# Seven block products in place of eight for the down projection of the first feed-forward block, in three chunks of six feature tiles and a plain chunk of four

## The chip, the cores and the metric

The kernel runs on one core of a Trainium2 chip. A core has a matrix engine (TensorE, PE in the profile; PEld is its loading of weights), a vector engine (VectorE, DVE), an activation engine (ScalarE, ACT), a general engine (GpSimd, POOL) and SyncE (SP), which only issues transfers. Each works through its own queue of instructions in order; they wait for each other by semaphores. SBUF holds operands, PSUM takes the sums of matmuls. The metric is the device time of one launch in microseconds.

## The reference

One step of a decoder trunk: a half-step SwiGLU feed-forward block, a mixer (pooling and a state-space scan), and a second feed-forward block, each behind an RMS norm, with residual adds. There are 512 prompt rows and 8 sample rows, 520 tokens in all, width 1024, feed-forward width 2816. Only the first feed-forward block is touched:

```python
def _swiglu(x, wg, wu, wd):
    return (jax.nn.silu(x @ wg) * (x @ wu)) @ wd
...
h = h + 0.5 * _swiglu(_rms_norm(h, ffn1_norm[l]), ffn1_w_gate[l], ffn1_w_up[l], ffn1_w_down[l])
```

The product with `wd` is the down projection: 2816 features in, 1024 out, for 520 tokens.

## The kernel before

Activations lie features on partitions, tokens along the free axis: `h` is 8 tiles of 128 features by 520 tokens. Tokens are split into two halves of 260 (`HB`). The 2816 inner features are 22 tiles of 128.

**Precision.** Each float32 operand is split into a rounded high part and a remainder, the low part. `mm3` (L122) forms a product as three matmuls: high by high, high by low, low by high. `split` (L102) makes the two parts of a weight: the high part by a copy on ACT (L107), the low part by a subtraction on DVE (L114), and, for a part of the columns called `late`, by ACT writing the negated high value (L110) and an accumulating DMA on POOL's queue adding the weight to it (L111).

**Gate and up products.** For each feature tile `f` the two weights (gate, up) and the two token halves form a 2 by 2 block problem, with the contraction in two halves as well. `Ffn.product` (L274) forms it by seven block products in place of eight (Winograd's variant of Strassen's scheme), numbered 1 to 7, each of 4 contraction tiles times 3 matmuls, so 84 matmuls to a tile. `load` (L255) fetches the weights and makes the combined ones: `s1` and `s2` by three additions on DVE (L266 to L268), then the splits of the plain and combined weights (`d1`, `e1`, `e2`, `d2`). The activations' seven combinations are made once, in `prep_pair` (L191), and kept in `xth` and `xtl`. Products that enter more than one output are copied out of PSUM to `ac` by ACT (L294) on the way. `gates` (L298) adds, scales by the norm factor and applies silu; `close` (L305) finishes the tile and splits the result into `g`, a high and a low part. The first two tiles of the block (`direct` = 2) are formed plainly during startup (`plain`, L226, `plain_out`, L241).

**Down products.** `rest` (L315) works through three chunks of 8, 8 and 6 feature tiles (`CHUNKS`). When a chunk's gates are done, `down` (L347) forms its share of the down projection for each of the 8 output tiles `d`: for each token half and each feature tile of the chunk one `mm3`, into two PSUM banks. `done` then scales the sum by -0.5 and the norm factor (L364) and adds it to `h` (L368). In the last chunk `after` also prepares the mixer's input of each finished output tile (`prep`, L141: a copy on ACT, a subtraction on DVE, L145, a square on ACT, L155, an add on DVE, L156).

**Order.** The gate product of the next chunk's first tiles is begun before a chunk's down products, so that TensorE is not left without work. Within these bounds the order of instructions on each engine is laid out ahead by a planner that runs on a cost model and takes work by priority and readiness. Buffers bound how far ahead it can go: two pairs of raw weights (`raw`), three high and low weight tiles (`whi`, `wlo`), two of each for combined weights (`sw`, `shi`, `slo`), three of `ac`, two of `tg`, and in PSUM two banks `A` and two pairs of banks `BE`. `g` has nine.

The second feed-forward block uses the same class, with `direct` = 1 and its own end (`down_by_half`).

Of the kernel before, what the change touches and what calls it, by code (L numbers as in the profile page):

```python
# [33 lines left out]
CHUNKS = (8, 8, 6)  # L34
# [28 lines left out]
def tile_trunk_step(ctx: ExitStack, tc: tile.TileContext, ins: dict, outs: dict):  # L63
# [120 lines left out]
    def scaled(gp, nb, norm, j, name):  # L184
        xg = gp.tile([P, 4, HB], F32, tag="g", bufs=nb, name=f"xg_{name}{j}")
        for d, out in ((j, xg[:, 0::3]), (j + KD // 2, xg[:, 1:3])):
            nc.scalar.activation(out=out, in_=h[:, d].rearrange("p (b t) -> p b t", b=2), func=AF.Copy,  # L187
                                 scale=v(norm, d))
        return xg

    def prep_pair(nx, gp, nb, xg, j, name):  # L191
        xth, xtl, _, _ = nx
        xd = gp.tile([P, 4, HB], F32, tag="g", bufs=nb, name=f"xd_{name}{j}")
        nc.vector.tensor_tensor(out=xd[:, 0:2], in0=xg[:, 0::2], in1=xg[:, 3:4].to_broadcast([P, 2, HB]),
                                op=ALU.subtract)
        nc.vector.scalar_tensor_tensor(out=xd[:, 2], in0=xd[:, 1], scalar=-1.0, in1=xg[:, 0], op0=ALU.mult,
                                       op1=ALU.subtract)
        nc.vector.scalar_tensor_tensor(out=xd[:, 3], in0=xd[:, 2], scalar=-1.0, in1=xg[:, 1], op0=ALU.mult,
                                       op1=ALU.subtract)
        for s, t in ((xg[:, 0:3], slice(0, 3)), (xd, slice(3, 7))):  # L200
            nc.scalar.copy(xth[:, j, t], s)
            nc.vector.tensor_tensor(out=xtl[:, j, t], in0=s, in1=xth[:, j, t].bitcast(F32), op=ALU.subtract)

    class Ffn:
# [4 lines left out]
        def __init__(self, nx, i, wx, gp, direct):  # L209
            self.nx, self.i, self.wx, self.gp, self.direct = nx, i, wx, gp, direct  # L210
            self.states = None
            self.w, self.A, self.BE, self.ac, self.g, self.tg, self.raw, self.banks, self.behind = ({} for _ in range(9))

# [12 lines left out]
        def plain(self, f, xg, j, us=(0, 1)):  # L226
            for u in us:
                if (f, u) not in self.banks:
                    n = f"P{self.i}_{f}{u}"
                    if f == 1 and u == 0:  # L230
                        bs = [ps[0].tile([P, 512], F32, tag="A", bufs=2, name=f"{n}{b}") for b in range(2)]
                    else:
                        t = ps[0].tile([P, 2, 512], F32, tag="BE", bufs=2, name=n)
                        bs = [t[:, 0], t[:, 1]]
                    self.banks[f, u] = bs
# [5 lines left out]
        def plain_out(self, f):  # L241
            tg = self.wx.tile([P, 2, HB], F32, tag="tg", bufs=2, name=f"tg{self.i}_{f}")
            g = self.g[f] = self.gp.tile([P, 2, 2, HB], F32R, tag="g", bufs=NG, name=f"g{self.i}_{f}")
# [4 lines left out]
            for b in range(2):  # L248
                nc.vector.scalar_tensor_tensor(out=tg[:, b], in0=self.banks[f, 1][b][:, :HB], scalar=-1.0, in1=tg[:, b],
                                               op0=ALU.mult, op1=ALU.mult)  # L250
            nc.scalar.copy(g[:, 0], tg)
            nc.vector.tensor_tensor(out=g[:, 1], in0=tg, in1=g[:, 0].bitcast(F32), op=ALU.subtract)
            return free.ins

        def load(self, f):  # L255
            i, wx, src = self.i, self.wx, ins[f"w{self.i}gu"]
            n = f"{i}_{f}"
            raw = raw_pair(n)
            nc.sync.dma_start(out=raw[:, 0], in_=src[2 * f])
            nc.sync.dma_start(out=raw[:, 1], in_=src[2 * f + 1])  # L260
            d1 = split(raw[:, 0], 1024, f"{n}a", wp, 3, ("whi", "wlo"), src[2 * f, :, 512:])
            s1 = wx.tile([P, 2, 512], F32, tag="sw", bufs=2, name=f"s1_{n}")
            s2 = wx.tile([P, 2, 512], F32, tag="sw", bufs=2, name=f"s2_{n}")
            up0 = raw[:, 1, :512].unsqueeze(1).to_broadcast([P, 2, 512])
            diag = bass.AP(up0.tensor, up0.offset - 1024, [up0.ap[0], (1536, 2), up0.ap[2]])
            nc.vector.tensor_tensor(out=s1, in0=diag, in1=up0, op=ALU.add)  # L266
            nc.vector.tensor_tensor(out=s2[:, 0], in0=s1[:, 1], in1=raw[:, 0, :512], op=ALU.add)
            nc.vector.tensor_tensor(out=s2[:, 1], in0=s2[:, 0], in1=raw[:, 0, 512:], op=ALU.add)  # L268
            e1 = split(s1.rearrange("p q c -> p (q c)"), 1024, f"{n}c", wx, 2, ("shi", "slo"))
            e2 = split(s2.rearrange("p q c -> p (q c)"), 1024, f"{n}d", wx, 2, ("shi", "slo"))  # L270
            d2 = split(raw[:, 1, 512:], 512, f"{n}b", wp, 3, ("whi", "wlo"), src[2 * f + 1, :, 512:])
            self.w[f] = {1: (d1, 0), 2: (d1, 4), 7: (e1, 0), 5: (e1, 4), 6: (e2, 0), 3: (e2, 4), 4: (d2, 0)}

        def product(self, f, p):  # L274
            js = range(KD // 2)
            if f not in self.A:
                with tc.issue_after(self.behind[f]) if f in self.behind else nullcontext():
                    self.load(f)
                n = f"{self.i}_{f}"
                self.A[f] = ps[0].tile([P, 512], F32, tag="A", bufs=2, name=f"A{n}")  # L280
                self.BE[f] = ps[0].tile([P, 2, 512], F32, tag="BE", bufs=2, name=f"BE{n}")
                self.ac[f] = [self.wx.tile([P, 2, HB], F32, tag="ac", bufs=3, name=f"ac{n}_{q}") for q in range(2)]
            slot, dst, opens = {1: (0, 0, True), 2: (1, 1, True), 5: (3, 2, True), 6: (5, 0, False),
                                3: (2, 2, False), 7: (4, 0, False), 4: (6, 0, False)}[p]
            out = self.A[f] if dst == 0 else self.BE[f][:, dst - 1]
            (whi, wlo), k0 = self.w[f][p]
            xth, xtl = self.nx[:2]
            for j in js:
                mm3(out[:, :HB], ws(whi, k0 + j), ws(wlo, k0 + j), xth[:, j, slot], xtl[:, j, slot], opens and j == 0,
                    j == KD // 2 - 1, skip_group_check=True)  # L290
            a, c = self.ac[f]
# [6 lines left out]
        def gates(self, f):  # L298
            tg = self.tg[f] = self.wx.tile([P, 2, HB], F32, tag="tg", bufs=2, name=f"tg{self.i}_{f}")
            nc.vector.tensor_tensor(out=tg, in0=self.BE[f][:, :, :HB], in1=self.ac[f][0], op=ALU.add)  # L300
            nc.vector.tensor_tensor(out=tg, in0=tg, in1=self.nx[3].rearrange("p (b t) -> p b t", b=2), op=ALU.mult)
            nc.scalar.activation(out=tg, in_=tg, func=AF.Silu)
            nc.vector.tensor_tensor(out=tg[:, 1], in0=self.ac[f][1][:, 0], in1=tg[:, 1], op=ALU.mult)

        def close(self, f):  # L305
            tg = self.tg[f]
            nc.vector.tensor_tensor(out=tg[:, 0], in0=self.A[f][:, :HB], in1=tg[:, 0], op=ALU.mult)
            g = self.g[f] = self.gp.tile([P, 2, 2, HB], F32R, tag="g", bufs=NG, name=f"g{self.i}_{f}")
            nc.scalar.copy(g[:, 0], tg)  # L309
            nc.vector.tensor_tensor(out=g[:, 1], in0=tg, in1=g[:, 0].bitcast(F32), op=ALU.subtract)  # L310
# [3 lines left out]

        def rest(self, before, last_chunk):  # L315
            lo = 0
            for c, n in enumerate(CHUNKS):
                hi = lo + n
                last = hi == KF
                for f in range(self.direct if c == 0 else lo + 1, hi if last else hi + 1):  # L320
                    self.step(f)
                if last:
                    self.product(KF - 1, 4)
                    with tc.high_priority():
                        self.close(KF - 1)
                    wd = before()
                else:
                    self.product(hi + 1, 1)
                    self.product(hi, 4)
                    self.close(hi)  # L330
# [4 lines left out]
                lo = hi  # L335

        def step(self, f):
            if f not in self.A:
                self.product(f, 1)
            if f - 1 not in self.g and f > self.direct:  # L340
                self.product(f - 1, 4)
                self.close(f - 1)
            for p in (2, 5, 6, 3, 7) if f == KF - 1 else (5, 6, 3, 7, 2):
                self.product(f, p)
            self.gates(f)
# [93 lines left out]
    wx1, g1 = pool("wx1", "right"), pool("g1", "right")  # L439
    ffn_psum("ppf1")  # L440
    nx1 = new_xt(xt1, "f1")
    ffn1 = Ffn(nx1, 1, wx1, g1, 2)
    xg1 = []
    for j in range(KD // 2):
# [4 lines left out]
        xg1.append(scaled(g1, NG, "ffn1_norm", j, "f1"))  # L449
# [4 lines left out]
        prep_pair(nx1, g1, NG, xg1[j], j, "f1")  # L454
    ffn1.plain_load(1)
    with tc.high_priority():
        ffn1.scales()
    for u in range(2):
        for j in range(KD // 2):
            ffn1.plain(1, xg1[j], j, (u,))  # L460
    with tc.high_priority():
        ffn1.behind[2] = ffn1.plain_out(0)
    ffn1.plain_out(1)
# [19 lines left out]
    def open_f2():  # L483
# [4 lines left out]
        f2["ffn"] = Ffn(new_xt(f2["xt"], "f2"), 2, f2["wx"], None, 1)  # L488

    def fin(d, b, hs):  # L490
# [5 lines left out]
        if j >= 0 and b:  # L496
            f2[j] = scaled(f2["xg"], 4, "ffn2_norm", j, "f2")

    def fill(j):
# [3 lines left out]
        prep_pair(f2["ffn"].nx, f2["xg"], 4, f2[j], j, "f2")  # L503
# [611 lines left out]
```

## Time and profile before

| | us |
|---|---|
| median of 3 runs | 1008.37 (1007.89 to 1009.1) |
| profiled execution | 1008.41 |
| its span, first to last instruction | 1006.5 |
| mean granted TensorE clock | 0.996 |

The first feed-forward block fills about the first 372 us of the span: the first matmul of startup starts at 5.25, the first down product at 112.0 and the last at 371.2, and the mixer's first matmul (`dt`) at 372.36. In rows of instructions the columns are the start, the duration, the engine, the line, the operation, the result and its operands, the shape and the count; in brackets stands the time for which the engine was idle before it and what ended that. In rows of busy time by stage the columns are the stretch, its length, then for PE, PEld, DVE, ACT and POOL the busy time and, in brackets, the number of instructions, then the granted TensorE clock, the DMA engines' share and GB/s. A matmul's printed duration (about 283 ns) is its latency; matmuls overlap, so what one costs is the distance from one start to the next.

### The profile page before, as it was taken

What the parts mean: (1) busy time and instruction counts of PE and PEld (TensorE: products, weight loads), DVE (VectorE), ACT (ScalarE), POOL (GpSimd) and SP (SyncE); (2) the same over time, 40 slices, a digit from 0 to 9 for tenths busy, and PEclk for the clock granted to TensorE, in tenths of its full rate; (3) what the DMA queues carried; (4) which work ended last, traced back from release to release, by engine and by line L of the source; (5) the groups of instructions that cost most, each with busy time, mean ns of one, the idle gap of its engine ahead of it and who ended that gap; (6) DMA issues with size and microseconds to landing.
All of it is one profiled execution on the core that took longest, in us unless ns stands there. A gap on an engine that the chain in (4) does not pass through costs nothing.

```text
span 1006.5 us, 19720 instructions
## 1 busy us (share of the span) xinstructions
PE 976.0 (97%) x7852; PEld 952.8 (95%) x7852; DVE 766.7 (76%) x1366; ACT 564.4 (56%) x961; POOL 157.3 (16%) x239
## 2 busy tenths in 40 slices
PE   7999999999999999999999999999999999999996
PEld 6899999999999999999899998899999999999995
DVE  7788556886468688789979987998857788477776
ACT  7677415765137455685754325677644676535653
POOL 0111001110011000156411000111212211122100
PEclk9999999999999999999999999999999999999998
DMA  5566424754345332263335322456646766556612
GB/s 185 166 167 163 111 99 116 178 137 117 126 110 135 93 124 97 90 192 100 121 122 159 117 86 95 127 131 175 140 139 185 210 151 165 131 179 171 144 64 85
DMA packets 53835, 135.97 MB, mean 135 GB/s; under 512 B 7720, under 2 KB 14824, under 8 KB 53744
## 3 DMA queue, kind: packets, MB, share of 16 engines
q1 hardware_dynamic: 38864, 103.78, 31.8%
q0 software_dynamic: 14880, 30.94, 16.0%
q8 instruction: 61, 1.00, 0.4%
q14 instruction: 30, 0.25, 0.1%
HBM read 127.36 MB, written 7.34 MB: 134 GB/s over the span
## 4 chain that ended last, share of the span: by engine, by line
PE 85%; DVE 6%; ACT 5%; issue 2%; DMA 2%; POOL 1%; SPq 0%; DVEq 0%; ACTq 0%; POOLq 0%
PE A L123 8%; PE A L126 7%; PE A L127 7%; PE dn L127 7%; PE dn L123 6%; PE dn L126 6%; PE BE L123 6%; PE BE L127 6%; PE BE L126 6%; PE P L238 3%; PE wo L123 2%; PE wo L126 2%; PE wo L127 2%; PE inz L123 2%; PE inz L127 2%
## 5 line engine op out<-in xcount | busy, mean ns | idle before, releaser
L123 PE MATMUL dn<-g,whi_1d 128*128 128x260 f32 x352 | 99.5, 283 | 1.8 <-ACT whi_1d L107 1.6
L126 PE MATMUL dn<-g,whi_1d 128*128 128x260 f32 x352 | 99.5, 283 | 0.0
L127 PE MATMUL dn<-g,wlo_1d 128*128 128x260 f32 x352 | 99.0, 282 | 0.0
L364 DVE SCALAR_TENSOR_TENSOR td<-dn,r_f 128x520 f32<-128x520 f32 x40 | 27.9, 699 | 91.7 <-PE dn L127 91.7
L127 PE MATMUL dn<-g,wlo_2d 128*128 128x260 f32 x256 | 72.8, 284 | 2.0 <-DVE wlo_2d L114 2.0
L123 PE MATMUL dn<-g,whi_2d 128*128 128x260 f32 x256 | 72.4, 283 | 0.1
L126 PE MATMUL dn<-g,whi_2d 128*128 128x260 f32 x256 | 72.3, 282 | 0.0
L123 PEld LDWEIGHTS dn<-g,whi_1d 128*128 128x128 f32 x352 | 66.1, 188 | 2.4 <-ACT whi_1d L107 2.0
L126 PEld LDWEIGHTS dn<-g,whi_1d 128*128 128x128 f32 x352 | 66.3, 188 | 0.0
L127 PEld LDWEIGHTS dn<-g,wlo_1d 128*128 128x128 f32 x352 | 66.1, 188 | 0.0
L107 ACT CAST whi_1d<-raw_1d 128x1024 fp32r<-128x1024 f32 (+1 forms) x24 | 23.4, 979 | 70.4 <-PE dn L126 62.2
L294 ACT COPY ac<-A 128x260 f32<-128x260 f32 x123 | 44.0, 371 | 17.1 <-PE A L127 17.1
L266 DVE TENSOR_TENSOR s<-raw 128x1024 f32<-128x1024 f32 x41 | 49.9, 1218 | 3.3 <-DMA raw<-in_w2gu 3.3
L238 PE MATMUL P<-xg_f,raw 128*128 128x260 f32 x192 | 45.6, 396 | 5.3 <-DMA raw<-in_w1gu 5.3
L127 PEld LDWEIGHTS dn<-g,wlo_2d 128*128 128x128 f32 x256 | 48.2, 188 | 2.6 <-DVE wlo_2d L114 2.6
L123 PEld LDWEIGHTS dn<-g,whi_2d 128*128 128x128 f32 x256 | 48.3, 189 | 0.3 <-ACT whi_2d L107 0.3
L126 PEld LDWEIGHTS dn<-g,whi_2d 128*128 128x128 f32 x256 | 48.2, 188 | 0.0
L238 PEld LDWEIGHTS P<-xg_f,raw 128*128 128x128 f32 x192 | 37.4, 198 | 11.2 <-ACT xg_f L187 5.2
L126 PE MATMUL wo<-catg,whi_wo 128*128 128x260 f32 x128 | 36.4, 285 | 1.3 <-DVE catg L972 1.3
L123 PE MATMUL wo<-catg,whi_wo 128*128 128x260 f32 x128 | 37.3, 292 | 0.3 <-DVE h L941 0.3
L310 DVE TENSOR_TENSOR g<-tg,g 128x520 fp32r<-128x520 f32 x41 | 28.6, 698 | 11.6 <-ACT g L309 11.6
L123 PE MATMUL inz<-xh_mx,whi_inz 128*128 128x260 f32 x128 | 36.8, 287 | 0.1
(1442 smaller groups left out, 4001.2 us busy)
## 6 DMA issues: line engine op xcount, KB each, us to landing
raw<-in_w2gu SPq DMA_DIRECT2D x44, 512.0 KB, 4.7
raw<-in_w1gu SPq DMA_DIRECT2D x42, 512.0 KB, 4.5
raw_1d<-in_w1d SPq DMA_DIRECT2D x16, 512.0 KB, 4.4
raw_2d<-in_w2d SPq DMA_DIRECT2D x16, 512.0 KB, 5.7
raw_wo<-in_w_out SPq DMA_DIRECT2D x12, 512.0 KB, 4.5
ab<-scr_acs SPq DMA_DIRECT2D x8, 512.0 KB, 4.4
h<-in_state_ssm SPq DMA_DIRECT2D x16, 256.0 KB, 4.1
raw_inz<-in_w_in SPq DMA_DIRECT2D x8, 512.0 KB, 4.3
```

The source lines that it names most:

```text
L107: nc.scalar.copy(h, src)
L123: first = nc.tensor.matmul(ps, whi, xhi, start=start, stop=False, **kw)
L126: nc.tensor.matmul(ps, whi, xlo, start=False, stop=False, **kw)
L127: nc.tensor.matmul(ps, wlo, xhi, start=False, stop=stop, **kw)
L238: nc.tensor.matmul(self.banks[f, u][b][:, :HB], ws(self.raw[f][:, u], j + 4 * q), xg[:, slot[q]], start=j == q == 0, stop=j == 3 and q == ...
L266: nc.vector.tensor_tensor(out=s1, in0=diag, in1=up0, op=ALU.add)
L294: nc.scalar.copy(keep, out[:, :HB])
L310: nc.vector.tensor_tensor(out=g[:, 1], in0=tg, in1=g[:, 0].bitcast(F32), op=ALU.subtract)
L364: nc.vector.scalar_tensor_tensor(out=t, in0=banks[d][:, :, :HB], scalar=-0.5, in1=self.nx[3].rearrange("p (b t) -> p b t", b=2), op0=ALU.mult,
```

## The change

The down projection of the first block is formed by the same seven products, for 18 of its 22 feature tiles. Chunks are now 6, 6, 6 and 4 tiles; `paired` = 3 says that the first three chunks go the new way. The second block keeps its chunks of 8, 8 and 6 and `paired` = 0.

- Within a paired chunk the feature tiles are worked in the order lo, lo+3, lo+1, lo+4, lo+2, lo+5. Two tiles in a row form a pair, "first" and "second": the two halves of the contraction of a block problem.
- The first tile's result is held in the tile `acc` (`gx`). When the second closes, `g_split` makes four differences on DVE and splits all seven combinations into high and low parts (three copies on ACT, three subtractions on DVE), in a tile `gt` of 14 x 260 columns; there are three of them, one for each pair of a chunk.
- A down step `(c, d)` takes the place of the plain down products of output tiles `d` and `d+1`: the two output tiles and the two token halves are the block problem. It goes through the same `load`, `product`, `gates` and `close` as a feature tile, with weights of 768 columns in place of 1024 and 3 contraction tiles in place of 4, so 63 matmuls in place of 72. Its `gates` and `close` scale and add to `h` instead of forming silu. There are 4 such steps to a chunk, 12 in all.
- The next chunk's first tile is stepped through before the down steps. Its result waits in `acc` until its partner closes; where the next chunk is the plain one (role "late"), `g_plain` splits it there.
- The last chunk has 4 feature tiles, and its down products are formed plainly, as before, with `after` for the mixer.
- At startup the plain tiles are 0 and 3, and the block's `xg` and `xd` tiles come from a pool of their own (`xo`), released before the pool of `gt` is opened.

```diff
-CHUNKS = (8, 8, 6)
+CHUNKS = {1: (6, 6, 6, 4), 2: (8, 8, 6)}
...
+                if c < paired:
+                    fs = [lo + q * (n // 2) + k for k in range(n // 2) for q in range(2)]
...
+        def g_homes(self, f):
+            t = self.tg[f]
+            if self.role(f) in ("first", "late"):
+                t = act.tile([P, NT], F32, tag="acc", name=f"gx{self.i}_{f}").rearrange("p (b t) -> p b t", b=2)
+                self.gx = t
+            self.out[f] = t
...
+        def g_split(self, f):
...
+            gx, go = self.gx, self.out[f]
+            self.gx = None
+            t = self.gt[f] = self.gp.tile([P, 14, HB], F32R, tag="gt", bufs=3, name=f"gt{self.i}_{f}")
+            xd = self.gp.tile([P, 4, HB], F32, tag="xd", name=f"gd{self.i}_{f}")
+            nc.vector.tensor_tensor(out=xd[:, 0], in0=gx[:, 0], in1=gx[:, 1], op=ALU.subtract)
+            nc.vector.tensor_tensor(out=xd[:, 1], in0=go[:, 1], in1=gx[:, 1], op=ALU.subtract)
+            nc.vector.scalar_tensor_tensor(out=xd[:, 2], in0=xd[:, 1], scalar=-1.0, in1=gx[:, 0], op0=ALU.mult,
+                                           op1=ALU.subtract)
+            nc.vector.scalar_tensor_tensor(out=xd[:, 3], in0=xd[:, 2], scalar=-1.0, in1=go[:, 0], op0=ALU.mult,
+                                           op1=ALU.subtract)
+            for x, q in ((gx[:, 0], 0), (go, slice(1, 3)), (xd, slice(3, 7))):
+                hi, lo = t[:, 0:7][:, q], t[:, 7:14][:, q]
+                nc.scalar.copy(hi, x)
+                nc.vector.tensor_tensor(out=lo, in0=x, in1=hi.bitcast(F32), op=ALU.subtract)
...
+        def load(self, k):
+            i, wx = self.i, self.wx
+            if isinstance(k, tuple):
+                c, d = k
+                fs = self.chunks[c]
+                n, src = f"{i}d{d}_{c}", ins[f"w{i}d"][d : d + 2, :, min(fs) * P : (max(fs) + 1) * P]
...
+            n = len(self.chunks[k[0]]) // 2 if isinstance(k, tuple) else KD // 2
+            for j in range(n):
+                if isinstance(k, tuple):
+                    t = self.gt[self.chunks[k[0]][2 * j + 1]]
+                    xhi, xlo = t[:, slot], t[:, 7 + slot]
...
+        def gates(self, k):
...
+            nc.vector.tensor_tensor(out=tg, in0=self.BE[k][:, :, :HB], in1=a, op=ALU.add)
+            if isinstance(k, tuple):
+                nc.vector.scalar_tensor_tensor(out=tg, in0=tg, scalar=-0.5, in1=r, op0=ALU.mult, op1=ALU.mult)
+                hd = self.halves(k[1])
+                nc.vector.tensor_tensor(out=hd, in0=tg, in1=hd, op=ALU.add)
+                nc.vector.scalar_tensor_tensor(out=c[:, 1], in0=c[:, 0], scalar=0.5, in1=r[:, 1], op0=ALU.mult,
+                                               op1=ALU.mult)
+                return
...
+        def close(self, k):
+            if isinstance(k, tuple):
+                _, c = self.ac[k]
+                nc.vector.scalar_tensor_tensor(out=c[:, 0], in0=self.A[k][:, :HB], scalar=0.5,
+                                               in1=self.nx[3][:, HALVES[0]], op0=ALU.mult, op1=ALU.mult)
+                hd = self.halves(k[1] + 1)
+                nc.vector.tensor_tensor(out=hd, in0=c, in1=hd, op=ALU.add)
+                return
...
         def rest(self, before, last_chunk):
...
+            for c, fs in enumerate(self.chunks):
+                last = c == len(self.chunks) - 1
+                ahead = [] if last else self.chunks[c + 1][:2]
+                for f in fs[self.direct if c == 0 else 1 :] + ahead[:1]:
                     self.step(f)
...
+                if c < self.paired:
+                    for d in range(0, KD, 2):
+                        self.step((c, d))
+                    continue
...
-    ffn1 = Ffn(nx1, 1, wx1, g1, 2)
+    ffn1 = Ffn(nx1, 1, wx1, None, 2, 3)
```

206 lines of the change are left out of this document (121 added, 85 removed).

## The prediction

> **What bounds the kernel now.** I read the page first, for who is busy and who ends last; then busy time by stage; then one step of the stage in question on VectorE, instruction by instruction.
>
> ```profile
> span 1006.5 us, 19720 instructions
> ...
> PE 976.0 (97%) x7852; PEld 952.8 (95%) x7852; DVE 766.7 (76%) x1366; ACT 564.4 (56%) x961; POOL 157.3 (16%) x239
> ...
> PE 85%; DVE 6%; ACT 5%; issue 2%; DMA 2%; POOL 1%; SPq 0%; DVEq 0%; ACTq 0%; POOLq 0%
> ```
>
> TensorE is busy for 97% and carries 85% of the chain of waits, so fewer matmuls are worth having wherever nothing else becomes late. The averages hide how the stages differ. Two rows of the busy time by stage (length, then PE, PEld, DVE, ACT, POOL, clock, DMA share, GB/s): the first spans two gate/up steps, the second is inside the plain down products.
>
> ```profile
> 75.06:95.26 20.20, 20.20 (x170) 20.20 (x169) 16.70 (x25) 14.18 (x24) 3.46 (x4) 1.00 0.65 157
> 130.00:160.00 30.00, 30.00 (x253) 30.00 (x253) 15.69 (x19) 5.79 (x6) 0.87 (x1) 1.00 0.31 106
> ```
>
> PE is full in both. But DVE is 83% busy in the first (16.70 of 20.20) and 52% in the second. The change turns the second kind of stage into one like the first. One gate/up step of DVE, in order of time:
>
> ```profile
> 75.06 1.23 DVE L114 TENSOR_TENSOR slo_6c<-s,shi_6c 128x1024 fp32r<-128x1024 f32 x1 [1.14 <-ACT shi_6c L107]
> 76.20 0.69 DVE L300 TENSOR_TENSOR tg<-BE,ac 128x520 f32<-128x520 f32 x1
> 76.81 1.22 DVE L266 TENSOR_TENSOR s<-raw 128x1024 f32<-128x1024 f32 x1
> 77.94 0.70 DVE L301 TENSOR_TENSOR tg<-tg,r_f 128x520 f32<-128x520 f32 x1
> 78.55 1.22 DVE L114 TENSOR_TENSOR slo_6d<-s,shi_6d 128x1024 fp32r<-128x1024 f32 x1
> 79.69 0.42 DVE L296 TENSOR_TENSOR ac<-ac 128x260 f32<-128x260 f32 x1
> 80.03 0.68 DVE L267 TENSOR_TENSOR s<-s,raw 128x512 f32<-128x512 f32 x1
> 80.63 0.42 DVE L303 TENSOR_TENSOR tg<-ac,tg 128x260 f32<-128x260 f32 x1
> 81.31 0.43 DVE L307 TENSOR_TENSOR tg<-A,tg 128x260 f32<-128x260 f32 x1 [0.26 <-PE A L127]
> 81.65 0.68 DVE L268 TENSOR_TENSOR s<-s,raw 128x512 f32<-128x512 f32 x1
> 82.27 0.69 DVE L114 TENSOR_TENSOR wlo_7a<-raw,whi_7a 128x512 fp32r<-128x512 f32 x1
> 83.32 0.70 DVE L310 TENSOR_TENSOR g<-tg,g 128x520 fp32r<-128x520 f32 x1 [0.36 <-ACT g L309]
> 85.16 1.23 DVE L114 TENSOR_TENSOR slo_7c<-s,shi_7c 128x1024 fp32r<-128x1024 f32 x1 [1.14 <-ACT shi_7c L107]
> ```
>
> The step repeats every 85.16 - 75.06 = 10.10 us, and PE runs 84 matmuls in it: 120.2 ns each. Two things matter on DVE. Back to back, an instruction costs the distance to the next start, less than its printed duration: 0.34 us for 260 columns, 0.61 for 520, 1.13 for 1024, so about 0.34 us + 1.03 ns for each column over 260; 384 columns come to 0.47 and 768 to 0.86. And 1.14 + 0.26 + 0.36 = 1.76 us of the step is DVE standing at the head of its queue, longest for the ACT copy of a combined weight. That is idle with work behind it; it costs nothing only while DVE has spare time.
>
> **The change, part by part.** *Matmuls removed.* In the plain down products the output tiles follow each other so:
>
> ```profile
> 133.95 0.70 DVE L364 SCALAR_TENSOR_TENSOR td<-dn,r_f 128x520 f32<-128x520 f32 x1 [2.94 <-PE dn L127]
> 134.69 0.70 DVE L368 TENSOR_TENSOR h<-td,h 128x520 f32<-128x520 f32 x1
> ...
> 139.69 0.70 DVE L364 SCALAR_TENSOR_TENSOR td<-dn,r_f 128x520 f32<-128x520 f32 x1 [3.17 <-PE dn L127]
> ```
>
> 139.69 - 133.95 = 5.74 us for 48 matmuls, 119.6 ns each, the same pace as above. Before: 22 feature tiles x 8 outputs x 2 halves x 3 = 1056 matmuls. After: 12 steps of 7 x 3 x 3 = 63, which is 756, and 4 x 8 x 2 x 3 = 192 plain, 948 in all. 108 fewer x 119.6 ns = **-12.9 us**.
>
> *Old joints.* Going into and through the first outputs of a plain chunk PE loses time now; rows of 25 us:
>
> ```profile
> 100.00:125.00 25.00, 23.55 (x192) 22.93 (x191) 14.02 (x20) 11.49 (x18) 1.73 (x2) 1.00 0.42 109
> 225.00:250.00 25.00, 24.33 (x200) 23.91 (x200) 15.29 (x23) 13.28 (x23) 2.60 (x3) 1.00 0.47 119
> 250.00:275.00 25.00, 24.22 (x202) 24.01 (x201) 10.74 (x13) 4.79 (x5) 0.00 (x0) 1.00 0.35 120
> ```
>
> The missing 1.45 and 0.67 + 0.78 = 1.45 us belong to two joints that no longer exist. **-2.9** (0 if the new joints lose as much; those are charged below).
>
> *A block-product down step.* PE: 63 x 120.2 ns = 7.57 us, where two plain outputs of six tiles took 72 x 119.6 = 8.61. DVE, by the costs above: combined weights 0.86 + 2 x 0.47, low halves 0.47 + 2 x 0.86, together 3.99; then adding the two kept parts 0.34, adding the bank 0.61, scaling 0.61, adding to h 0.61, two 260-column scalings 0.68, and the last add 0.61, together 3.46. Sum 7.45 us of 7.57: DVE is as full as PE. Dependent neighbours cost more, as td and h above show (start to start 0.74, not 0.61), by 0.13 each when nothing stands between them. The work can be packed: scaling and adding to h are urgent for nobody but the next joint, and could fill the 1.14 us in which DVE now stands waiting for ACT. The bounds for a step are 0 (all packed) and 7.45 + 1.14 - 7.57 = 1.02 us (the wait stays and nothing fills it). That neither side must win is shown by two stretches where DVE is as full:
>
> ```profile
> 300.00:310.00 10.00, 10.00 (x85) 10.00 (x85) 9.42 (x16) 7.22 (x12) 1.34 (x2) 1.00 0.61 151
> ...
> 650.00:660.00 10.00, 8.97 (x70) 8.34 (x70) 9.58 (x14) 5.80 (x11) 1.58 (x3) 1.00 0.53 147
> ```
>
> At 94% PE lost nothing; at 96%, elsewhere, it lost a tenth. The first is the nearer row, since it stands in this feed-forward block, so I take a quarter of the upper bound, 0.25 us x 12 = **+3.0** (0 to 12.2).
>
> *The other engines in that step.* ACT casts or copies 3 x 768 + 384 + 2 x 384 = 3456 columns and keeps four parts:
>
> ```profile
> 84.08 1.05 ACT L107 CAST shi_7c<-s 128x1024 fp32r<-128x1024 f32 x1 [0.52 <-PE BE L126]
> ```
>
> At 1.05 us per 1024 that is 3.5 us and some 1.5 for the four 260-column copies: 5.0 of 7.57, no bound. The two loads and two accumulating loads move 0.79 + 0.39 = 1.18 MB in 7.57 us, 156 GB/s, where the gate/up steps run at 157 with PE full. SP and POOL issue two transfers a step, as in a gate/up step. All at nothing.
>
> *Splitting the activations.* Each pair of feature tiles adds four 260-column differences (1.36) and low parts of 260, 520 and 1040 columns (2.09), and drops two of 520 (1.22): +2.23 us of DVE per pair, 16.70 + 2.23 = 18.93 of 20.20. It all falls after the second tile closes, so the step behind a pair needs 16.70 / 2 - 0.61 + 3.45 = 11.2 us of DVE against PE's 10.1. Inside a chunk the next step (7.7) takes the rest up. At a chunk's end it cannot, since the full down steps follow, and their third block reads exactly this split. Bounds for the three chunk ends 0 and 3 x 3 us (1.1 over, plus the 1.76 of standing, carried along); I take 1 each, **+3.0**. Plain startup pair: DVE gains 2.85 us there,
>
> ```profile
> 25.00:50.00 25.00, 24.16 (x155) 22.07 (x154) 19.54 (x27) 15.21 (x25) 3.62 (x4) 1.00 0.59 167
> ```
>
> and has 5.5 us idle in this row: **+0.8** (0 to 2).
>
> *The last chunk, four tiles instead of six.* Its DVE work, from the last gate to the mixer:
>
> ```profile
> L145 DVE SCALAR_TENSOR_TENSOR xl_mx<-h,xh_mx 128x260 fp32r<-128x260 f32 x16 | 7.6, 484 | 0.7 <-ACT xh_mx L144 0.7
> L371 DVE TENSOR_TENSOR h<-td,h 128x260 f32<-128x260 f32 x16 | 6.1, 422 | 0.0
> L156 DVE TENSOR_TENSOR acc_mx<-acc_mx,sq_mx 128x260 f32<-128x260 f32 x14 | 5.9, 422 | 0.0
> L114 DVE TENSOR_TENSOR wlo_1d<-raw_1d,whi_1d 128x768 fp32r<-128x768 f32 x6 | 5.7, 952 | 0.3 <-ACT whi_1d L107 0.3
> L364 DVE SCALAR_TENSOR_TENSOR td<-dn,r_f 128x520 f32<-128x520 f32 x8 | 5.5, 697 | 3.0 <-PE dn L127 3.0
> L114 DVE TENSOR_TENSOR wlo_inbc<-raw_inbc,whi_inbc 128x1024 fp32r<-128x1024 f32 x1 | 1.2, 1224 | 0.3 <-ACT whi_inbc L107 0.3
> ```
>
> Per output, back to back: 0.61 + 2 x 0.34 + 2 x 0.40 + 2 x 0.34 + 0.86 = 3.63 us, under PE's 36 x 119.6 = 4.31. With four tiles only the weight's low half shrinks (to 0.60): 3.37 us, over PE's 24 x 119.6 = 2.87. DVE sets the pace: 8 x 0.50 = 4.0 us, and 6.3 if two mixer weights (1.13 each) still go between. The mixer's first products read the last output tile, so this is on the path. **+5.0** (4.0 to 6.3).
>
> How the clock takes a pause, at the kernel's end, where PE stops:
>
> ```profile
> 996.00:1000.00 4.00, 1.12 (x4) 0.30 (x3) 2.58 (x5) 1.05 (x3) 0.00 (x0) 0.92 0.17 60
> 1000.00:1003.00 3.00, 0.00 (x0) 0.00 (x0) 2.53 (x4) 0.00 (x0) 0.00 (x0) 0.50 0.45 150
> ```
>
> It falls to half within some microseconds of idle, while the joints' rows above hold 1.00 at losses under 1.5 us. A rule of the Trainium skill speaks against a stall of 5 us here (TensorE: Matmul & The Clock Gate, Part 1: The HAM clock gate): after an idle window of some 3.4 us TensorE's clock is halved until it has been busy as long; an estimate from it is 3.4 / 2 = 1.7 us more, if the 5.0 come in one piece. The rows agree with it. Broken over eight outputs, the sum stays.
>
> **Sum:** -12.9 - 2.9 + 3.0 + 3.0 + 0.8 + 5.0 = -4.0 us. The profiled execution took 1008.41 us (span 1006.5, 1.9 around it), the median is 1008.37. Forecast **1004.4 us**.
>
> **Rivals.** *VectorE becomes the bound* (the other side). DVE keeps its queue order of a gate/up step and stands 1.14 us for the combined weight in every down step, while the elastic work stays behind it: 12 x 1.02 = 12.2 us. Pairs then need 18.93 + 2 x 1.14 = 21.2 us against 20.2, up to 1 us x 8. Then -15.8 + 12.2 + 0.8 + 5.0 = +2.2, to +10.2 with the pairs: 1010.6 to 1018.6, middle 1014.6. For it: 7.45 of 7.57 leaves 0.12 us, and the 650 row. Against it: the 300 row. It decides from 0.8 us lost per down step on, where 12 x 0.83 = 10.0 uses up the gain left after tail and startup. *All is covered*: chunk ends and down steps lose nothing and the tail its least: -15.8 + 4.0 = -11.8, 996.6. Against it: three places at once must pack without a gap. *A wash*: losses of some 8 to 12 us beside the tail, within 2 us of before, 1008.4. *The issue order shifts*: the order on each engine comes from a planner, and new tiles may push a load or a split late elsewhere in the block, as the old joints (1.4 us each) show that it can; five such joints beyond the sum give 1004.4 + 7 = 1011.4. The matmul count itself follows from the loops, so that part isn't in doubt.
>
> **How the numbers follow.** Forecast 0.36 (about 1000 to 1006), covered 0.12, wash 0.13, VectorE 0.33, order 0.06. A measurement tells 0.2% (2 us) from no change. So faster 0.48, same 0.13, slower 0.39. Cases of both signs hold most of the chance: the forecast's own range is 1000 to 1006.4; the range given, 996.5 to 1017, leaves out part of the covered case and the top of the VectorE one.
>
> **What would show it.** 108 fewer matmuls; a down step's period (63 matmuls) of 7.6 to 8.0 us, where 8.4 or more means VectorE; DVE's idle for ACT's combined weight in those steps, near 0 against 1.14; PE waits in the last chunk's outputs named after DVE's td or h, 4 to 6 us; clock 1.00 throughout the block. The forecast is wrong if down steps take over 8.4 us, if gate/up steps grow past 10.3, or if the tail costs nothing.

## The result, and the profile after

| | before | changed |
|---|---|---|
| median, us | 1008.25 (4 runs, 1007.89 to 1009.1) | 999.76 (4 runs, 996.79 to 1000.87) |
| profiled execution, us | 1008.41 | 1000.70 |
| its span, us | 1006.5 | 998.8 |

The ratio is 0.991, 95% interval 0.9886 to 0.9934. In a second session it was 0.9901 (0.9881 to 0.9921; median 998.44 of 6 runs, profiled execution 998.23). The change gains 8.5 and 10.5 us, more than twice the 4.0 forecast. The page of the changed kernel:

```profile
span 998.8 us, 19958 instructions
...
PE 965.1 (97%) x7744; PEld 941.1 (94%) x7744; DVE 830.9 (83%) x1519; ACT 614.5 (62%) x1074; POOL 178.0 (18%) x263
...
PE 84%; DVE 8%; ACT 3%; DMA 3%; issue 1%; POOL 0%; SPq 0%; DVEq 0%; ACTq 0%
```

TensorE has 7852 - 7744 = 108 matmuls less. VectorE has 64 us more to do and its share rises from 76% to 83%. TensorE still carries most of the chain of waits (84%, and VectorE 8% where it had 6%). Now the down steps, where the forecast feared most: VectorE's rows of three of them, each at the low half of the first combined weight, and the busy time of the two steps from the first to the third (columns as before).

```profile
94.51 0.96 DVE L114 TENSOR_TENSOR slo_1d_0c<-s_1d,shi_1d_0c 128x768 fp32r<-128x768 f32 x1 [0.77 <-ACT shi_1d_0c L107]
102.04 0.96 DVE L114 TENSOR_TENSOR slo_1d_0c<-s_1d,shi_1d_0c 128x768 fp32r<-128x768 f32 x1 [0.58 <-ACT shi_1d_0c L107]
109.56 0.96 DVE L114 TENSOR_TENSOR slo_1d_0c<-s_1d,shi_1d_0c 128x768 fp32r<-128x768 f32 x1
```

```profile
94.51:109.56 15.05, 15.05 (x128) 15.05 (x127) 14.47 (x25) 10.45 (x20) 3.46 (x4) 1.00 0.72 176
```

The period is 7.53 and 7.52 us, which is 63 matmuls at 119.4 ns. TensorE is full while VectorE is 96% busy. The time for which VectorE stands at the head of its queue, waiting for ACT's copy, shrinks from 0.77 to 0.58 to nothing: as VectorE falls behind, it no longer arrives early. In the second of the two steps it works through its 13 instructions in 7.52 us, without a gap. So a wait of this kind, 1.14 us in a gate step before, is spare time here, not a fixed cost. Where the down steps go over into gate steps, one row of 10 us at each chunk's end is not full; this is the first:

```profile
120.00:130.00 10.00, 9.49 (x79) 9.27 (x79) 9.50 (x16) 6.27 (x10) 1.73 (x2) 1.00 0.62 152
```

0.5 us, three times, where each old joint showed 1.45. But busy time, which counts a matmul's whole printed duration, shows too little of such a loss, as the starts show. First the longest wait of an old joint, in the kernel before, then the one in the row above:

```profile
121.35 0.28 PE L126 MATMUL dn<-g,whi_1d 128*128 128x260 f32 x1
122.40 0.39 PE L123 MATMUL dn<-g,whi_1d 128*128 128x260 f32 x1 [0.77 <-ACT whi_1d L107]
122.63 0.28 PE L126 MATMUL dn<-g,whi_1d 128*128 128x260 f32 x1
```

```profile
122.33 0.28 PE L127 MATMUL A<-xth_f,wlo_9a 128*128 128x260 f32 x1
123.12 0.39 PE L123 MATMUL A<-xth_f,shi_9d 128*128 128x260 f32 x1 [0.51 <-ACT ac L364]
123.34 0.28 PE L126 MATMUL A<-xtl_f,shi_9d 128*128 128x260 f32 x1
```

From 121.35 to 122.63 two matmuls take 1.28 us, which take 0.24 at the pace of 120 ns: 1.04 are lost where the bracket says 0.77. Counted in this way over all matmuls, each of the two old joints lost 2.25 us, and each of the three new chunk ends loses 1.0.

Then the end of the block. First what TensorE waits for in the block behind its startup, the longest first; then VectorE's queue around the last outputs; then busy time by pieces of 2 us.

```profile
PE dt L737 <- DVE td L463: 3.1, 1, 3.1
PE A L123 <- ACT ac L364: 1.5, 3, 0.5
PE dn L123 <- ACT gt L248: 0.6, 1, 0.6
```

```profile
359.11 1.22 DVE L114 TENSOR_TENSOR wlo_inbc<-raw_dt,whi_inbc 128x1024 fp32r<-128x1024 f32 x1
360.24 0.48 DVE L145 SCALAR_TENSOR_TENSOR xl_mx<-h,xh_mx 128x260 fp32r<-128x260 f32 x1
360.64 0.76 DVE L470 TENSOR_TENSOR h<-td,h 128x260 f32<-128x260 f32 x2
361.32 0.69 DVE L463 SCALAR_TENSOR_TENSOR td<-dn,r_f 128x520 f32<-128x520 f32 x1
...
362.67 1.22 DVE L114 TENSOR_TENSOR wlo_inbc<-raw_inbc,whi_inbc 128x1024 fp32r<-128x1024 f32 x1
...
367.05 0.48 DVE L145 SCALAR_TENSOR_TENSOR xl_mx<-h,xh_mx 128x260 fp32r<-128x260 f32 x1
```

```profile
358.00:360.00 2.00, 1.08 (x9) 0.87 (x8) 2.00 (x5) 1.78 (x5) 0.00 (x0) 1.00 0.00 0
360.00:362.00 2.00, 0.00 (x0) 0.00 (x0) 2.00 (x6) 1.27 (x5) 0.00 (x0) 1.00 0.28 57
362.00:364.00 2.00, 1.84 (x11) 1.49 (x12) 2.00 (x5) 0.75 (x2) 0.00 (x0) 0.64 0.97 379
364.00:366.00 2.00, 2.00 (x11) 1.63 (x10) 2.00 (x7) 1.00 (x3) 0.00 (x0) 0.50 0.79 293
366.00:368.00 2.00, 2.00 (x17) 1.62 (x15) 1.88 (x7) 1.91 (x4) 0.23 (x1) 1.00 0.00 0
```

TensorE's last down product starts at 358.8 (371.2 before) and then stands 3.1 us, the mixer's first matmul waiting for a scaling that VectorE reaches only at 361.32, behind a mixer weight and older work. VectorE has no gap there. Behind this idle the granted clock falls to half until 366. The mixer's first input product starts at 368.3, where before it was 376.8. So of the 12.4 us gained up to the last down product, 3.8 are given back before the mixer's first input product.

### The profile page after: what moved, and what is told of

Its sections match the earlier page's. It is cut to its first block, busy times and chain, and to the rows that moved or that the text cites. A ratio compares the mean times of both kernels' runs of the same rounds, so it can differ in the third digit from the quotient of the medians.

```text
span 998.8 us, 19958 instructions
## 1 busy us (share of the span) xinstructions
PE 965.1 (97%) x7744; PEld 941.1 (94%) x7744; DVE 830.9 (83%) x1519; ACT 614.5 (62%) x1074; POOL 178.0 (18%) x263
## 4 chain that ended last, share of the span: by engine, by line
PE 84%; DVE 8%; ACT 3%; DMA 3%; issue 1%; POOL 0%; SPq 0%; DVEq 0%; ACTq 0%
PE A L123 8%; PE A L126 7%; PE A L127 7%; PE BE L127 6%; PE BE L123 6%; PE BE L126 6%; PE P L296 3%; PE dn L127 2%; PE dn L126 2%; PE dn L123 2%; PE wo L123 2%; PE wo L127 2%; PE wo L126 2%; PE A1d L126 2%; PE A1d L127 2%; PE A1d L123 2%
## 5 line engine op out<-in xcount | busy, mean ns | idle before, releaser
L123 PE MATMUL dn<-g,whi_2d 128*128 128x260 f32 x256 | 72.3, 282 | 0.0
L123 PEld LDWEIGHTS dn<-g,whi_2d 128*128 128x128 f32 x256 | 48.3, 189 | 0.0
L463 DVE SCALAR_TENSOR_TENSOR td<-dn,r_f 128x520 f32<-128x520 f32 x24 | 16.7, 698 | 33.6 <-PE dn L127 33.6
L107 ACT CAST whi_2d<-raw_2d 128x1024 fp32r<-128x1024 f32 (+1 forms) x18 | 18.5, 1026 | 31.6 <-PE dn L126 16.7
L123 PE MATMUL wo<-catg,whi_wo 128*128 128x260 f32 x128 | 37.3, 292 | 0.3 <-DVE h L1043 0.3
L123 PE MATMUL inz<-xh_mx,whi_inz 128*128 128x260 f32 x128 | 36.8, 287 | 0.0
L123 PE MATMUL inx<-xh_mx,whi_inx 128*128 128x260 f32 x128 | 36.4, 284 | 0.0
L127 PE MATMUL wo<-catg,wlo_wo 128*128 128x260 f32 x128 | 36.4, 284 | 0.0
L127 PE MATMUL inz<-xh_mx,wlo_inz 128*128 128x260 f32 x128 | 36.2, 283 | 0.0
L127 PE MATMUL inx<-xh_mx,wlo_inx 128*128 128x260 f32 x128 | 36.2, 282 | 0.0
L126 PE MATMUL inz<-xl_mx,whi_inz 128*128 128x260 f32 x128 | 36.2, 282 | 0.0
L126 PE MATMUL inx<-xl_mx,whi_inx 128*128 128x260 f32 x128 | 36.1, 282 | 0.0
L942 ACT ACTIVATE so<-br,sxdt 128x128 f32<-128x128 f32 x64 | 20.5, 391 | 24.5 <-DMA br<-scr_bc 18.1
```

What stands on the lines that cost most here:

```text
L107: nc.scalar.copy(h, src)
L123: first = nc.tensor.matmul(ps, whi, xhi, start=start, stop=False, **kw)
L126: nc.tensor.matmul(ps, whi, xlo, start=False, stop=False, **kw)
L127: nc.tensor.matmul(ps, wlo, xhi, start=False, stop=stop, **kw)
L463: nc.vector.scalar_tensor_tensor(out=t, in0=banks[d][:, :, :HB], scalar=-0.5, in1=self.nx[3].rearrange("p (b t) -> p b t", b=2), op0=ALU.mult,
L942: nc.scalar.activation(out=o[:, q], in_=br, func=AF.Copy, scale=sxdt[:, j, b : b + 1]))
```

## The experiments

The base is the changed kernel. Its executions of the second session took 997.7 to 1003.6 us, too wide a spread for some of the differences below. So a place in the trace stands beside the medians: how long after the first matmul of the second gate step that reads a combined weight (tile `shi_4c`, or `shi_3c` where tile 3 is formed there) the mixer's first input product starts. In the base:

```profile
L123 PE MATMUL BE<-xth_f,shi_4c x4: 277/282/286, 48.9 to 49.9; 128*128 128x260 f32 x4
```

```profile
L123 PE MATMUL inbc<-xh_mx,whi_inbc x64: 278/282/474, 368.3 to 392.5; 128*128 128x260 f32 x64
```

That is 319.4 us (328.9 in the kernel before), and it repeated to 0.1 us. What lies outside of it varies by itself: that first matmul starts between 47.5 and 48.9 us in the profiles of the kernels below, although the startup's code differs in two of them alone, and from the first input product to the end it takes 630.6, 628.1 and 629.8 us in three profiles of the same instructions (the base twice, and the kernel with the high priority, see there), 627.8 to 632.6 in all. Differences in parentheses are to the base, 998.44 us and 319.4 us; the median of the kernel before was 1008.4 to 1009.3 in the sessions of these runs.

### The base again

> The changed kernel once more, as the base of the other runs. Theory: TensorE sets the pace in the paired chunks, and the end of the block costs 4.8 us (3.1 us of idle before the mixer's first matmul, then some 1.7 us because the clock is granted at half); so about 999.5 us, with the half clock between 358 and 368 us of the span in the profile again. Rival: the half clock was an accident of one execution; then it is gone here and the time is 998 or less.

998.44 us (997.67 to 1003.63, 6 runs), place 319.4. The waits in the block behind the startup are the same to 0.1 us, and the clock in the row from 360 to 370 is again 0.83. The half clock was no accident of one execution. The profiled span is 2.4 us shorter than the first one; 2.0 of it come later: in the second block TensorE waited 3.9 us for weights' low parts in the first profile and 1.9 here.

### The new chunks, but plain down products

```diff
-    ffn1 = Ffn(nx1, 1, wx1, None, 2, 3)
+    ffn1 = Ffn(nx1, 1, wx1, None, 2, 0)
```

> The new chunks (6, 6, 6, 4), but all down products plain, so 1056 matmuls. Theory (the loss at the end belongs to the last chunk's four tiles): 1008.3 + 4.8 for the end + 1.4 for one joint more = 1014.5 us, with a wait of 2 to 4 us before the mixer and a granted clock under 1 there. Rival (the loss at the end belongs to what the block products leave behind on VectorE): no such wait, 1008 to 1010 us.

1015.7 us, place 336.8 (+17.4), ratio 1.0062 (1.0047 to 1.0077): the chunks alone make the kernel slower. The same wait stands before the mixer, and the same fall of the clock behind it:

```profile
PE dt L737 <- DVE td L463: 3.1, 1, 3.1
```

```profile
376.00:378.00 2.00, 0.00 (x0) 0.00 (x0) 2.00 (x5) 1.25 (x3) 0.00 (x0) 1.00 0.10 18
378.00:380.00 2.00, 1.32 (x7) 1.03 (x8) 2.00 (x4) 1.27 (x4) 0.00 (x0) 0.52 0.93 293
```

So the stall is the last chunk's four tiles, not something the block products leave behind. And in equal chunks the block products are worth 1015.7 - 998.4 = 17.3 us, 17.4 by the place: 13.0 of matmuls and, by the distances from start to start, 3.6 of joints (three of 2.2 us here, 1.0 in the base) and 0.6 at the first products of the last chunk.

### More work for VectorE in every down step

```diff
+                for q in range(2):
+                    w = self.wx.tile([P, 2, HB], F32, tag="more", bufs=1, name=f"more{n}_{q}")
+                    nc.vector.tensor_tensor(out=w, in0=tg, in1=r, op=ALU.mult)
                 hd = self.halves(k[1])
```

With `range(1)` in the second kernel.

> Two more products of 520 columns on VectorE in every down step (1.22 us a step, into a tile that nobody reads). Theory (VectorE just fits, 7.45 of 7.53 us): the step grows to some 8.6 us where nothing carries the rest, 12 x 1.1 = 13 us and 1012 us; if the gate steps take up what the down steps leave (84.8 + 4 x 1.22 = 89.7 of 90.4 us in a chunk), 3 to 8 us more, 1003 to 1008. Rival (VectorE has room that the sum does not show): within 1 us of the changed kernel.

> One more product of 520 columns (0.61 us of VectorE) in every down step, where two gave 9.8 us more than the changed kernel. Theory (0.1 us of room in a step and some room in the gate steps beside it): 12 x 0.5 = 6.0 us at most, 2 to 5 likely, 1000.5 to 1003.5. Rival (the loss comes from the planner's order with two, not from the load): under 1 us more, or as much as with two.

With two, 1008.24 us (+9.8), place 328.4 (+9.0). With one, 1005.66 (+7.2), place 325.7 (+6.2). The added work is 14.6 and 7.3 us, of which 61% and 85% appear in the place. Steps with one more product, VectorE's rows:

```profile
93.35 0.96 DVE L114 TENSOR_TENSOR slo_1d_0c<-s_1d,shi_1d_0c 128x768 fp32r<-128x768 f32 x1 [0.78 <-ACT shi_1d_0c L107]
100.93 0.96 DVE L114 TENSOR_TENSOR slo_1d_0c<-s_1d,shi_1d_0c 128x768 fp32r<-128x768 f32 x1
108.81 0.95 DVE L114 TENSOR_TENSOR slo_1d_0c<-s_1d,shi_1d_0c 128x768 fp32r<-128x768 f32 x1
```

The first period is still 7.58, the next 7.88: the standing time is used up one step earlier, and from there VectorE has no gap. TensorE runs up to 3 matmuls ahead in these steps and loses its time behind them (16.66 of 18.00 us busy from 108 to 126). VectorE just fits; the room is smaller than the sum of 7.45 in 7.57 us says. The first product costs 0.5 us a step, theory's upper end, the second only 0.2, so the loss does not follow the load alone; how much the planner's other order adds or hides is not separated. Of the median's +7.2 the profile places 6.2.

### Six plain tiles at the end

```diff
-CHUNKS = {1: (6, 6, 6, 4), 2: (8, 8, 6)}
+CHUNKS = {1: (4, 6, 6, 6), 2: (8, 8, 6)}
```

> Chunks of 4, 6, 6 and 6: the last plain chunk is six tiles again and the first block-product chunk has four. 12 matmuls more (1.4 us); its four down steps have 42 matmuls (5.0 us) but need 2.8 + 3.5 = 6.3 us of VectorE. Theory (four plain tiles make the stall; VectorE limits a down step once its sum passes TensorE's): no wait over 1 us before the mixer and no half clock, -3.9 us; the four short steps cost 1.2 us each, less what the gate steps carry, +1 to +4.9; in sum 997 to 1001, and the steps' period over 5.6 us. Rival (VectorE is no limit in down steps): period 5.0 us and 996 us.

1002.62 us (+4.2), place 321.0 (+1.6). No half clock, and the wait before the mixer is the old one:

```profile
PE dt L737 <- DVE td L463: 0.9, 1, 0.9
```

But in the short down steps (42 matmuls, 5.0 us) VectorE needs more than TensorE, and sets the period:

```profile
71.84 0.69 DVE L114 TENSOR_TENSOR slo_1d_0c<-s_1d,shi_1d_0c 128x512 fp32r<-128x512 f32 x1 [0.15 <-PE BE1d L126]
...
77.51 0.68 DVE L114 TENSOR_TENSOR slo_1d_0c<-s_1d,shi_1d_0c 128x512 fp32r<-128x512 f32 x1
...
83.10 0.68 DVE L114 TENSOR_TENSOR slo_1d_0c<-s_1d,shi_1d_0c 128x512 fp32r<-128x512 f32 x1
```

5.67 and 5.59 us, in which VectorE has no gap. TensorE runs ahead at first, with 46 and 45 matmuls in these periods, and then stands:

```profile
83.00:90.00 7.00, 4.31 (x27) 3.30 (x26) 7.00 (x14) 3.10 (x6) 1.73 (x2) 1.00 0.85 216
```

By the starts, the end of this chunk loses 5.6 us where a chunk's end of the base loses 1.0, and 1.4 go to the 12 matmuls more; the gain at the end of the block, 5.2 us, does not pay for them. One wait of 1.0 us among these is for a transfer (`wlo_1d_0b`), so not all of it is VectorE's. What the median loses beyond the place, 2.6 us, lies behind the block and is not explained. The rival of the forecast, VectorE as the bound, is true here and not in the base, where a step's sum does not pass TensorE's.

### The stall at the end: order or load

Four attempts to make it smaller. First the order alone, high priority for the scaling that frees the banks:

> In the last chunk's outputs the scaling that frees the PSUM banks gets high priority, so that no mixer weight stands ahead of it; VectorE's work is the same. Rival to the load theory (the order makes the stall): the wait before the mixer falls from 3.1 to 1.2 us, the clock stays 1.00, 2 to 3.5 us under the changed kernel. Load theory: the mixer's first products wait for the last preparation instead, which ends no sooner; within 1 us of the changed kernel, 998 to 999.5.

999.33 us (+0.9), place 319.4 (+0.0). The wait stays 3.1 us. But this run decides nothing: the order it asks for did not come about. On every engine the instructions stand in the order of the base, and the last scaling still comes behind the mixer weight:

```profile
357.94 1.21 DVE L114 TENSOR_TENSOR wlo_inbc<-raw_dt,whi_inbc 128x1024 fp32r<-128x1024 f32 x1
...
360.15 0.69 DVE L464 SCALAR_TENSOR_TENSOR td<-dn,r_f 128x520 f32<-128x520 f32 x1
```

So it is the base once more, and another order is not tested. What the base's trace shows for the load: the low halves of the last outputs' weights follow each other at 345.99, 349.35 and 352.72, that is one output in 3.36 us of VectorE where TensorE needs 2.87, and the mixer's first input product starts 0.75 us after the end of VectorE's last preparation (367.53).

Then the load. The additions of the squares on GpSimd:

```diff
-            nc.vector.tensor_tensor(out=acc[:, hs], in0=acc[:, hs], in1=sq[:, :n], op=ALU.add)
+            eng = nc.gpsimd if name.startswith("mx") else nc.vector
+            eng.tensor_tensor(out=acc[:, hs], in0=acc[:, hs], in1=sq[:, :n], op=ALU.add)
```

> The 14 additions of the squares in the mixer's preparation go to GpSimd in place of VectorE: 14 x 0.34 = 4.8 us less for VectorE between the last gate and the mixer. Theory (VectorE's load in the last chunk makes the stall): the wait of the mixer's first matmul falls from 3.1 us to under 1, the clock stays 1.00, the time is 2 to 5 us under the changed kernel, 995 to 998. Rival: the stall comes from the order in VectorE's queue (a mixer weight ahead of the last scaling), then the wait stays over 2 us and the time within 1 us. Third: GpSimd's additions are slower and the norm waits for them, 0 to 3 us longer.

1003.83 us (+5.4), place 321.7 (+2.3), and a wait of 4.3 us: a miss. Groups of VectorE's and GpSimd's instructions from 340 us on (shape, count, busy time, mean ns of one):

```profile
L145 DVE SCALAR_TENSOR_TENSOR xl_mx<-h,xh_mx 128x260 fp32r<-128x260 f32 x16 | 10.1, 647 | 0.1
L471 DVE TENSOR_TENSOR h<-td,h 128x260 f32<-128x260 f32 x16 | 7.9, 520 | 0.0
...
L157 POOL TENSOR_TENSOR acc_mx<-acc_mx,sq_mx 128x260 f32<-128x260 f32 x14 | 14.1, 1017 | 16.9 <-ACT sq_mx L155 16.9
```

The same VectorE instructions take 484 and 424 ns in the base. With 16 x (163 + 96) ns and the weights' low halves (819 ns in place of 687) VectorE lost as much as the 4.8 us it was spared.

The low halves of the last chunk's weights by ScalarE and an accumulating transfer:

```diff
-                    units[d] = load_unit(ins[f"w{self.i}d"][d, :, lo * P : hi * P], n * P, f"{self.i}d{d}_{c}")
+                    src, name = ins[f"w{self.i}d"][d, :, lo * P : hi * P], f"{self.i}d{d}_{c}"
+                    raw = raw_tile(name)[:, : n * P]
+                    nc.sync.dma_start(out=raw, in_=src)
+                    units[d] = split(raw, n * P, name, wp, 3, ("whi", "wlo"), src if after is not None else None)
```

> The low parts of the last chunk's weights (8 of 512 columns, 0.60 us each on VectorE) are made as in the gate steps: ScalarE writes the negated high part and an accumulating transfer adds the weight. 4.8 us less for VectorE, no arithmetic on GpSimd. Theory (VectorE's load in the last chunk makes the stall): the wait before the mixer falls from 3.1 to under 1.5 us, no half clock, 2 to 4.5 us under the changed kernel, 994 to 997 us. Rival (the order in VectorE's queue makes it): the wait stays at 2 us or more, within 1 us of the changed kernel. Third: the transfers land too late for the matmuls (a longer chain for a buffer), then new waits for them and no gain.

1003.95 us (+5.5), place 322.7 (+3.3). The wait before the mixer is 0.9 us and the clock holds 1.00, as the load theory says, but the down products wait for their weights instead:

```profile
PE dn L127 <- DMA wlo_1d<-in_w1d: 4.6, 4, 2.0
```

The squares summed by TensorE with float32 matmuls:

```diff
-        sumsq(acc, d, hs, name)
+        b = at[1]
+        if d == 0:
+            sums[b] = bank(f"psr_mx{b}")[:, :HB]
+        sq = tmp.tile([P, HB], F32, tag="ta", name=f"sq_{name}")
+        nc.scalar.activation(out=sq, in_=h[:, d, hs], func=AF.Square)
+        nc.tensor.matmul(sums[b], ones, sq, start=d == 0, stop=d == KD - 1)
...
-    rstds(nx2[0], "mx")
```

> The squares of the mixer's norm are summed by TensorE as they come (14 float32 matmuls with ones more, each into the norm's bank) in place of 14 additions on VectorE: 4.8 us less for VectorE after the last gate, nothing more for GpSimd or the transfers. Theory (VectorE's load in the last chunk makes the stall): the wait before the mixer falls from 3.1 to under 1.5 us and the mixer's first input product starts 2 to 4.5 us earlier than 368.3; 994 to 996.5 us. Rival: the float32 sums take TensorE as long as the stall did (14 x 0.22 = 3.1 us, the pace of the plain startup products); then within 1 us of the changed kernel, 998 to 999.5.

1005.46 us (+7.0), place 322.8 (+3.4). VectorE has gaps again and the longest wait of the end is 1.2 us, but TensorE's last down product starts 5.4 us later, counted like the place: its trace shows 32 records for the 16 sums. The work was moved onto the other full engine.

### The price of the half clock

```diff
         prep(nx2[0], "mix_norm", d, hs, f"mx{d}{b}")
+        if (d, b) == (KD - 1, 1):
+            warm, xw = bank("warm"), nx2[0][0]
+            for q in range(24):
+                nc.tensor.matmul(warm[:, :HB], xw[:, 0, :P], xw[:, q % 4, HALVES[0]], start=True, stop=True)
```

> 24 more matmuls into a spare bank behind the last down product, which nobody reads, so that TensorE is not idle in the stall (24 x 0.12 = 2.9 us). It prices the half clock by itself. If the clock's fall costs time: granted clock 1.00 between 358 and 370 us and 1.7 us less than the changed kernel, 996.7. If the mixer waits for VectorE's last preparation anyway (which ends at 367.5 us in the changed kernel): clock 1.00, but the mixer's first input product still starts at 368 and the time is within 0.5 us, 998.4.

The clock stays 1.00 and the place is 319.7 (+0.3): nothing is gained. The 24 matmuls went between the down products (346 to 355 us), not behind them, so they fill and shift the idle rather than follow it, and the run alone is no clean price. The kernel with two more products gives one: the same wait stands there, but the clock stayed at 1.00 behind it.

```profile
PE dt L740 <- DVE td L466: 3.1, 1, 3.1
```

```profile
371.00:373.00 2.00, 2.00 (x17) 1.78 (x18) 2.00 (x5) 0.57 (x2) 0.00 (x0) 1.00 0.96 369
```

From the last down product to the first input product it takes 9.5 us in that kernel and in the base, with the full clock and with the half. So the half clock costs nothing here. It hides behind VectorE: with the full clock TensorE waits 1.0 us more for VectorE's preparations (`PE dt L739 <- DVE xl_mx L145`), and in all three kernels the first input product starts 0.75 us after the end of VectorE's last preparation. The kernel of this run took 1004.55 us (+6.1); its profile (1001.12) shows 2.9 of that, behind the block: the mixer's gate products end at 538.2 against 535.3 in the base. Why stays open.

### Two mixer weights out of the way

```diff
-        wh, wl = load_unit(src, D, f"in{name}")
+        wh, wl = load_unit(src, D, f"in{name}", name in ("bc0", "bc1"))
```

`load_unit` passes its source to `split` as `late` there, so that ScalarE and an accumulating transfer make the low parts.

> The low parts of the mixer's first two input weights, which stand in VectorE's queue between the last chunk's outputs (2 x 1.13 us), are made by ScalarE and an accumulating transfer; they are needed only behind the mixer's first products. 2.3 us less for VectorE before the last preparation. Theory (VectorE's total in the last chunk sets the mixer's start): the first input product starts 1.5 to 2.3 us before 368.3, at 366 to 367 us, the time is 1 to 2.5 us under the changed kernel, 996 to 997.5. Rival: TensorE then waits for the transfers or for something else on the way, and the start stays at 368 or later.

995.84 us (994.86 to 996.18, 4 runs), place 317.4 (-2.1), ratio 0.9878 (0.9861 to 0.9894), the lowest median of all. The interval overlaps the base's (0.9881 to 0.9921), so the gain rests on the place. What TensorE waits for before the mixer, and the mixer's first input products (shortest, median and longest duration in ns, first and last start):

```profile
PE dt L737 <- DVE td L463: 1.5, 1, 1.5
```

```profile
L123 PE MATMUL inbc<-xh_mx,whi_inbc x64: 278/282/472, 365.1 to 389.3; 128*128 128x260 f32 x64
```

2.1 us gained, for 2.3 us of VectorE's work, as theory says. The start lies 3.2 us before the base's, but 1.1 of that are startup. The clock holds 1.00. The transfers that came late for the down products are in time for these: they are read only behind the mixer's first matmuls. The run takes this work off VectorE; whether it would do to leave it there, behind the last preparation, has not been run.

## Why the prediction was right, and where its size was off

The sums here count from the place's first matmul, with what a wait costs read from start to start.

- *Matmuls removed, -12.9.* Held: 108, at 119.4 ns in the down steps.
- *Old joints, -2.9.* Mis-sized: they cost 4.5. The idle that the forecast read from rows of 25 us is less than the time lost, because a matmul's printed duration, longer than its share of the pace, counts as busy.
- *Down steps, +3.0 (0 to 12.2).* Mis-sized, the largest error: they cost nothing. The sum on VectorE (7.45 us, measured 7.52, against TensorE's 7.52) was right, and so was the remark that the work can be packed. Wrong was to charge a quarter of the standing time as if it would stay; it was spare time, and it shrank to nothing.
- *Chunk ends, +3.0.* The size was met, by some luck: 1.0 each. The mechanism, VectorE's backlog, makes 0.2 of each (the low half `slo_9c` ends at 118.59, and the matmul that waits for it starts at 118.64); 0.8 are the wait for a copy on ACT that the next product into the same bank needs.
- *Startup, +0.8 (0 to 2).* Not shown. The base's second gate step starts 0.9 us later than before, but in the other kernels with the same startup it starts 0.5 earlier to 0.8 later; the change is lost in that spread.
- *The last chunk, +5.0 (4.0 to 6.3).* Held in size, 5.2, of which 3.8 belong to its mechanism, a little under the lower bound. The mechanism was right, and the plain kernel in the new chunks shows it by itself: VectorE's 3.36 us against 2.87 per output make 3.8 us behind the last down product. The mixer's weights, which the upper bound counted, are a part of it: taking them out gave 2.1 us back. The other 1.4 are of another kind: the chunk's first products now wait longer for the last tile's split (`PE dn L123 <- ACT gt L248`).
- *The clock.* It fell behind 3.1 us of idle in one piece; from 362 to 366 us that is 0.36 x 2 + 0.50 x 2 = 1.7 us of lost clock, the estimate's very number. The idle is close to the 3.4 us of the rule weighed there (the Trainium skill, TensorE: Matmul & The Clock Gate, Part 1: The HAM clock gate). The traces agree with it in part: behind the same 3.1 us the clock stayed at 1.00 in the kernel with two more products. The 1.7 us added nothing to the time: the stretch up to the mixer's first input product is as long in that kernel.

Together: -13.0 - 4.5 + 3.0 + 1.4 + 3.8 and 0.2 less for the pace of the matmuls make -9.5, as the place says (328.9 to 319.4), and between the 8.5 and 10.5 of the medians. The forecast's -4.0 missed 3.0 in the down steps, 1.6 in the joints and 0.8 in the startup. The rival in which VectorE sets the pace was wrong for steps of six tiles, where it is exactly as full as TensorE, and right for steps of four.

## What to carry to other kernels

Idle time at the head of an engine's queue can be spare time, as in these steps, where it shrank as soon as the engine fell behind; add up the busy time of one period, from one start to the next, and compare that with the period, before pricing the waits. Read what a wait costs the pacing engine from start to start, not from its idle time. Look in the trace whether an edit changed what it was to change, before its time is taken for an answer. Where a block shrinks the pacing engine's work, look at its end too: the outputs' finishing work did not shrink with it, and what was hidden for six tiles was bare for four. Relief there has to go to something that is neither full nor late: GpSimd, TensorE and a transfer needed at once all gave it back, a transfer needed later did not.

## What the runs showed of the hardware that was not expected

Elementwise work on GpSimd slows VectorE beside it: 14 additions of 260 columns took 1017 ns each there, and VectorE's instructions with both operands in SBUF in the same stretch went from 484 to 647 and from 424 to 520 ns, while its scalings out of PSUM stayed at 688 (696 in the base). And the granted clock fell to 0.5 behind an idle of 3.1 us, for about 3.4 us, in both profiles of the base, but stayed at 1.00 behind the same 3.1 us in the kernel with two more products.
